# Probabilities' low halves against V's high columns only, a smaller planned cost, and 27 unread products at the end

## Chip, cores and metric

The kernel runs on one core of one Trainium2 chip. The metric is device time in microseconds, the median of several runs. Lower is better.

## The reference

Two layers, 256 positions, width 1024, one sequence. Each layer is, in short:

```python
h = rms_norm(x, gain)
proj = h @ w_in                       # 1024 -> 9808 columns, all branches at once
# qa ka va ga | qb kb vb gb | qc kc vc gc | indexer | forget logit | merge logits
oa = moba_attention(rope(qa), rope(ka), va) * silu(ga)     # 8 heads of 64
ob = dsa_attention(rope(qb), rope(kb), vb, indexer) * silu(gb)
oc = forgetting_attention(qc, kc, vc, log_f) * silu(gc)
y = stack([oa, ob, oc]) @ w_branch    # three matrices 512 -> 1024
merged = sum(sigmoid(merge_logit) * y)
x = x + merged @ w_out
```

At the end stands one more rms_norm. At 256 positions the MoBA branch is plain causal attention; the DSA branch keeps 64 keys per query; the forgetting branch adds a bias to the logits. In all three, one head computes softmax(scores) @ V with V of 64 columns.

## The kernel before

**Precision by halves.** TensorE works on fp32r operands. Every float32 operand is split into a high half (an fp32r copy, made on ACT) and a low half (the difference, made on DVE), and a product A x B is made as high x high + low x high + high x low. For V both halves lie side by side: `v[:, t, hd]` has 128 columns for head hd and key tile t, the first 64 the high half, the last 64 the low half. The transposed probabilities of a head lie in `ph` (high) and `pl` (low), 384 columns each: columns 0 to 255 are key tile 0 against all 256 queries, columns 256 to 383 key tile 1 against the last 128 queries (the rest is masked by causality).

**The attention of a pair of heads** (class Pair, function attend): scores (L566 to L568), bias, exponential and normalisation (L629 to L644), transposes of the probabilities (L656), their split (L659, L661), and then the products with V in `av` (L671 to L674). For each of the two heads, four products add into one 128 x 256 region `ov` of a PSUM bank: rows 0 to 63 collect what meets V's high columns, rows 64 to 127 what meets V's low columns. In the kernel before, the fourth product (low probabilities, key tile 0) takes all 128 columns of V, the third (low probabilities, key tile 1) only the first 64. Function gated then adds the upper and the lower 64 rows (L687 on ACT, then DVE) and multiplies by the gate. There are 3 mixers x 4 pairs x 2 layers = 24 such pairs, 48 heads.

**Projections.** Most of TensorE's work is in mm_ops (L403): weights come by DMA into three raw buffers, are split into wh (ACT, L358) and wl (DVE, L362), and are multiplied with hTh and hTl, the two halves of the transposed, normalised input. Key tiles of a pair's k are written in block form as bd (L704 on ACT, L705 on DVE).

**The order.** Nothing runs in program order. Every piece of work is an operation with an engine, a cost in ns, tokens that it reads and writes, and a key (a due number). A planner (Plan.run) simulates the engines: it takes the engine with the earliest possible start, and there the operation with the smallest key, advances that engine by the operation's cost, and emits the instruction. So the costs written into the kernel decide the order of instructions on each engine and in SP's queue of loads, not what they take on the chip. All groups of mm_ops write one token, k_main, and so keep their order among themselves; attention pieces, norms and transposes go between them as keys and planned times have it. The planned cost of `av` is 820 ns.

**The end.** The output projection w_out closes a layer. In the last layer its last part is cut in two halves of 256 columns; after each follow the residual on DVE (L1032), sum of squares, the final norm (L526 to L551) and the output's DMA. When the output has landed, SP and POOL collect all engines in a closing barrier (L1063).

Of the kernel before, what the change touches and what calls it, by code (L numbers as in the profile page):

```python
# [29 lines left out]
C_ID, C_UT, C_MASK, C_ROPE, C_END = 0, 128, 256, 640, 1664  # L30
# [11 lines left out]
MARGIN = 200.0  # L42
# [191 lines left out]
def hybrid_trunk(ctx, tc, x, norm_gain, w_in, forget_bias, w_branch, w_out, final_gain, consts, out):  # L234
    nc = tc.nc
    PE, ACT, DVE, POOL = nc.tensor, nc.scalar, nc.vector, nc.gpsimd
# [13 lines left out]
    def T(b):  # L250
        return b.slot[1]


    def pe(fn, cost, reads, writes, key, name="", margin=0.0, touch=()):
        o = plan.op([("PE", cost, fn)], reads, writes, key, 0.0, name, touch)
        o.margin = margin
        return o

    def act(fn, n, ps, reads, writes, key, name="", extra=0.0, touch=()):
        return plan.op([("ACT", t_act(n, ps) + extra, fn)], reads, writes, key, 0.0, name, touch)  # L260
# [22 lines left out]
    hTh = pool.tile([128, KC, S], F32R, name="hTh")  # L283
    hTl = pool.tile([128, KC, S], F32R, name="hTl")
# [5 lines left out]
    cst = pool.tile([128, C_END], F32, name="cst")  # L290
    ident = cst[:, C_ID:C_ID + 128]
# [17 lines left out]
    k_id, k_rope, k_gT, k_bdz, k_cst, k_fb, k_wf, k_widx, k_lf, k_cs, k_main = (Tok() for _ in range(11))  # L309
# [103 lines left out]
    hT_all = [[t for tl in k_hT[p] for t in tl] for p in range(2)]  # L413
# [158 lines left out]
    class Pair:  # L572
# [46 lines left out]
        def attend(self, key):  # L619
            bs = [self.bias(h, key) for h in range(2)]  # L620
            s0, s1 = scores(self.q, self.k, self.kt, key)
            es, ke = [], []
            for h in range(2):
                b, bt, bb = bs[h]
                e, st = Buf("e"), Buf("st")
                kt = [Tok(), Tok()]
                parts = ((0, 0, 128, s0), (1, 128, 256, s1))
                for t, a, n, s in parts:
                    dve(lambda t=t, a=a, n=n, s=s, e=e, st=st, b=b, h=h: DVE.tensor_tensor_reduce(  # L629
                        T(e)[:, a:a + n], T(s)[:, h * n:(h + 1) * n], b()[:, a:a + n], 1.0, 3e38, ALU.add, ALU.min,  # L630
                        T(st)[:, t:t + 1]), n, [s, bt[t]], [kt[t]], key, "max", touch=[e, st] + bb)
                for t, a, n, s in parts:
                    act(lambda t=t, a=a, n=n, e=e, st=st: ACT.activation(  # L633
                        T(e)[:, a:a + n], T(e)[:, a:a + n], AF.Exp, bias=T(st)[:, t:t + 1], scale=-1.0,
                        accum_out=T(st)[:, 2 + t:3 + t]), n, False, [], [kt[t]], key, "exp", 185.0, touch=[e, st])
                for t, a, n, s in parts:
                    dve(lambda t=t, st=st: DVE.reciprocal(T(st)[:, 4 + t:5 + t], T(st)[:, 2 + t:3 + t]), 1, [], [kt[t]],
                        key, "recip", 75.0, touch=[st])

                    def on_act(t=t, a=a, n=n, e=e, st=st):  # L640
                        ACT.activation(T(e)[:, a:a + n], T(e)[:, a:a + n], AF.Copy, scale=T(st)[:, 4 + t:5 + t])

                    def on_dve(t=t, a=a, n=n, e=e, st=st):
                        DVE.tensor_scalar(T(e)[:, a:a + n], T(e)[:, a:a + n], T(st)[:, 4 + t:5 + t], None, op0=ALU.mult)  # L644
                    plan.op([("DVE", 129.0 + 0.52 * n, on_dve), ("ACT", t_act(n, False) + 93.0, on_act)], [], [kt[t]],
                            key, 0.0, "normalise", touch=[e, st]).port = True
                es.append(e)
                ke.append(kt)
            ph, pl = Buf("pth"), Buf("ptl")
            kp = [[Tok(), Tok()] for _ in range(2)]  # L650
            for h in range(2):
                ps = Buf("t")

                def tr(h=h, ps=ps):
                    for i in range(3):
                        PE.transpose(T(ps)[:, i * 128:(i + 1) * 128], T(es[h])[:, i * 128:(i + 1) * 128], ident)  # L656
                pe(tr, 330.0, ke[h] + [k_id], [ps], key, "pT", MARGIN, touch=[es[h]])
                src = lambda ps=ps: T(ps)[:, :384]
                act(lambda h=h, src=src: ACT.activation(T(ph)[:, h], src(), AF.Copy), 384, True, [ps],  # L659
                    [kp[h][0]], key, "pT", touch=[ph])  # L660
                dve(lambda h=h, src=src: DVE.tensor_tensor(T(pl)[:, h], src(), T(ph)[:, h].bitcast(F32), op=ALU.subtract),  # L661
                    384, [ps, kp[h][0]], [kp[h][1]], key, "pT", touch=[ph, pl])
            o = Buf("o")
            v = V[self.vi]

            def av():
                for h in range(2):
                    hd = 2 * self.p + h
                    ov = T(o)[:, h * S:(h + 1) * S]
                    a, b = slice(0, 256), slice(256, 384)  # L670
                    PE.matmul(ov, v[:, 0, hd], T(ph)[:, h, a], start=True, stop=False)  # L671
                    PE.matmul(ov[:, 128:], v[:, 1, hd], T(ph)[:, h, b], start=False, stop=False)
                    PE.matmul(ov[:64, 128:], v[:, 1, hd, :64], T(pl)[:, h, b], start=False, stop=False)
                    PE.matmul(ov, v[:, 0, hd], T(pl)[:, h, a], start=False, stop=True)  # L674
            kv = [t for p in k_V[self.vi] for t in p]
            pe(av, 820.0, kv + [ph, pl] + [t for h in kp for t in h], [o], key, "av", MARGIN)
            self.o, self.o_key = o, key
            if hasattr(self, "g"):
                self.gated()
# [312 lines left out]
    for l in range(L):  # L992
        gates = {}
        if l == 0:
            first_v()
        else:
            v_units(l, "a", 0)
        u, ps = unit_b("kwf", lambda k: win_k(l, k), 80)
        kb, ktoks = ev_kwf(l, ps, u)
        wf_cols(l, u + 1)  # L1000

        def index_unit(p):
            u, ps = unit_b(f"qi{p}", lambda k: win_b(l, COL["qi"] + (p // 2) * 256, p % 2, k))
            index_scores(p, ps, kb, ktoks, u)
            if p == 3:
                select(u + 3, 2.0)
        first = [lambda p=p: index_unit(p) for p in range(4)] + mixer(l, "a", 0, 0)
        for f in between(first, m_of(l, 0, gates, range(8)) + m_of(l, 2, gates, range(NC1))):
            f()
        v_units(l, "c", 1)  # L1010
        for f in between(mixer(l, "c", 1, 1), alternate(y_of(l, 0, 0, 0, gates, range(8)), m_of(l, 2, gates, range(NC1, 8)))):
            f()
        v_units(l, "b", 0)
        for f in between(mixer(l, "b", 0, 0), alternate(y_of(l, 2, 1, 1, gates, range(8)), m_of(l, 1, gates, range(NB1)))):
            f()
        for f in m_of(l, 1, gates, range(NB1, 8)) + y_of(l, 1, 0, 2, gates, range(8)):
            f()
        last = l + 1 == L
        if last:
            dma(lambda: nc.sync.dma_start(acc.rearrange("p k c -> p (k c)")[:, :D],  # L1020
                                          final_gain.rearrange("(o d) -> o d", o=1).to_broadcast([128, D])),
                512 * D, [], [k_fg] + k_acc, units[0], "final gain")
        for hh in range(2):
            gets = [lambda k, i=i: rows_a("O", w_out, l, hh * 512, i, k) for i in range(4)]
            for t in range(2):
                ra = [lambda k, p=p: [k_mg[k][p]] for p in range(2)]
                cols = [(0, 256), (256, 256)] if last and hh + t == 2 else [(0, 512)]
                for i, (c, n) in enumerate(cols):
                    u, ps = unit_a(f"o{hh}{t}", gets, t, mA[0], mA[1], ra, c, n)
                    c += hh * 512  # L1030
                    o = xs[t][:, c:c + n]
                    dve(lambda o=o, ps=ps, n=n: DVE.tensor_tensor(o, o, T(ps)[:, :n], op=ALU.add), n, [ps], [k_x[t][hh]],  # L1032
                        u - 4, "res")
                    if last:
                        final_part(t, c, n, hh + i, u - 4, i == 1)
                if last and hh == 1:
                    final_norm(t, orr[t], u - 4, 1 + len(cols))
                elif hh == 1:
                    norm_to_hT(l + 1, t, u - 2)
    PLAN_T.append(plan)  # L1040
    PLAN_T[0] = plan.run({"PE": 0.0, "ACT": 0.0, "DVE": 0.0})

# [24 lines left out]
```

## Time and profile before

| | |
|---|---|
| runs | 639.62, 639.74, 640.1 us (median 639.74) |
| profiled execution, span from first to last instruction | 639.9 us |
| granted TensorE clock, mean | 0.996 |
| TensorE products (PE) / weight loads (PEld) busy | 624.9 / 595.6 us |
| DVE / ACT / POOL busy | 546.7 / 396.3 / 89.8 us |
| DMA | 105.56 MB, 165 GB/s on average |

The profiled execution's own time is known as its span alone; the three runs lie on both sides of it. Products on TensorE are pipelined, so their recorded lengths overlap: a busy share near 100% says that TensorE was never long without a product, not how fast products follow each other. What one product costs is the distance to the start of the next one.

### The profile page before, as it was taken

Reading aid. Unit: us, or ns where it says so; the run is one execution under the profiler, and the core shown is the slowest. Engines: PE = TensorE matmul, PEld = TensorE weight load, DVE = VectorE, ACT = ScalarE, POOL = GpSimd, SP = SyncE. Lnnn points to the kernel's source line nnn. Section 1 sums busy time; section 2 is a strip of 40 time slices with the busy share of each in tenths; the row PEclk is TensorE's granted clock in tenths of the full one; section 3 lists DMA queues with packets and bytes.
Section 4 is the critical chain, followed back from the end, with each engine's and each line's share of the span. In section 5 each row is a group of like instructions: output and inputs, shape, how many; then the busy total and the mean of one; then the engine's idle time right before and its main releaser. Section 6 shows DMA issues by size and latency. Waiting matters only on the chain.

```text
span 639.9 us, 12574 instructions
## 1 busy us (share of the span) xinstructions
PE 624.9 (98%) x4836; PEld 595.6 (93%) x4836; DVE 546.7 (85%) x1331; ACT 396.3 (62%) x802; POOL 89.8 (14%) x96
## 2 busy tenths in 40 slices
PE   7999989999999999999999999999999999999996
PEld 6899989999998999999889999998999889999985
DVE  7799999885969989998588999989587898999873
ACT  5675475765755658485386555767457564858641
POOL 1242131100000221200004403020000003221000
PEclk9999999999999999999999999999999999999999
DMA  8745628455382552656445634565635354552711
GB/s 292 241 142 186 198 71 291 133 165 165 104 276 84 165 173 93 198 163 233 153 134 194 198 105 160 162 201 164 205 125 198 102 171 158 165 165 99 264 34 67
DMA packets 93853, 105.56 MB, mean 165 GB/s; under 512 B 4320, under 2 KB 82400, under 8 KB 93792
## 3 DMA queue, kind: packets, MB, share of 16 engines
q1 hardware_dynamic: 93504, 104.36, 49.8%
q8 instruction: 38, 0.62, 0.4%
q10 hardware_dynamic: 288, 0.39, 0.2%
q14 instruction: 23, 0.19, 0.1%
HBM read 103.69 MB, written 1.05 MB: 164 GB/s over the span
## 4 chain that ended last, share of the span: by engine, by line
PE 82%; DVE 12%; issue 2%; ACT 2%; DMA 1%; SPq 0%; POOL 0%; POOLq 0%; DVEq 0%; ACTq 0%
PE proj L403 70%; DVE wl L362 4%; PE t L656 2%; PE proj L947 2%; PE s L566 1%; PE s L568 1%; DVE isc L801 1%; PE s L567 1%; DVE e L629 1%; PE o L674 1%; DMA x<-in_x_dram 1%; DVE t L800 1%; ACT wh L358 1%; PE o L671 1%; DVE isc L780 1%
## 5 line engine op out<-in xcount | busy, mean ns | idle before, releaser
L358 ACT ACTIVATE wh<-raw 128x1024 fp32r<-128x1024 f32 (+1 forms) x190 | 199.0, 1054 | 133.7 <-PE proj L403 107.6
L362 DVE TENSOR_TENSOR wl<-raw,wh 128x1024 fp32r<-128x1024 f32 (+1 forms) x190 | 238.4, 1264 | 39.3 <-ACT wh L358 38.3
L403 PE MATMUL proj<-hTh,wh 128*128 128x256 f32 (+1 forms) x1040 | 252.4, 278 | 1.1 <-DVE bd1l L705 0.6
L403 PE MATMUL proj<-hTl,wh 128*128 128x256 f32 (+1 forms) x1040 | 251.6, 277 | 0.0
L403 PEld LDWEIGHTS proj<-hTh,wh 128*128 128x128 f32 (+1 forms) x1040 | 194.6, 187 | 2.1 <-DVE bd1l L705 0.8
L403 PEld LDWEIGHTS proj<-hTl,wh 128*128 128x128 f32 (+1 forms) x1040 | 194.6, 187 | 0.6
L403 PE MATMUL proj<-hTh,wl 128*128 128x256 f32 (+1 forms) x1040 | 163.4, 279 | 0.0
L403 PEld LDWEIGHTS proj<-hTh,wl 128*128 128x128 f32 (+1 forms) x1040 | 139.8, 188 | 1.3
L449 POOL TENSOR_TENSOR rsh<-rsh,cst 128x256 f32<-128x256 f32 (+1 forms) x42 | 37.1, 884 | 406.4 <-DVE rsh L448 406.4
L633 ACT ACTIVATE e<-e,st 128x128 f32<-128x128 f32 x96 | 42.7, 446 | 20.0 <-DVE st L629 19.9
L451 POOL TENSOR_TENSOR rr<-rr,rsh 128x256 f32<-128x256 f32 (+1 forms) x42 | 47.5, 1131 | 15.7 <-DVE rr L450 12.9
L403 PE MATMUL proj<-wh,v 128*128 128x512 f32 (+1 forms) x144 | 35.5, 368 | 0.0
L403 PE MATMUL proj<-wh,hTh 128*128 128x512 f32 x80 | 32.7, 409 | 1.2 <-DVE bd0l L705 0.6
L403 PE MATMUL proj<-og0h,wh 128*128 128x256 f32 x128 | 32.4, 277 | 0.0
L403 PE MATMUL proj<-og0l,wh 128*128 128x256 f32 x128 | 32.3, 277 | 0.0
L403 PE MATMUL proj<-wh,hTl 128*128 128x512 f32 x80 | 31.5, 394 | 0.0
L403 PEld LDWEIGHTS proj<-wh,v 128*128 128x128 f32 x144 | 25.2, 188 | 4.7
L659 ACT ACTIVATE pth<-t 128x384 fp32r<-128x384 f32 x48 | 22.1, 484 | 8.2 <-PE t L656 8.1
L661 DVE TENSOR_TENSOR ptl<-t,pth 128x384 fp32r<-128x384 f32 x48 | 25.6, 551 | 1.5 <-ACT pth L659 1.3
L403 PE MATMUL proj<-og0h,wl 128*128 128x256 f32 x128 | 25.0, 277 | 0.0
L403 PE MATMUL proj<-wl,hTh 128*128 128x512 f32 x80 | 24.9, 392 | 0.0
L403 PEld LDWEIGHTS proj<-og0h,wh 128*128 128x128 f32 x128 | 24.1, 188 | 0.4 <-DVE mth L848 0.2
(190 smaller groups left out, 1010.7 us busy)
## 6 DMA issues: line engine op xcount, KB each, us to landing
raw<-in_w_in_dram SPq DMA_DIRECT2D x74, 1024.0 KB, 5.0
raw<-in_w_branch_dram SPq DMA_DIRECT2D x24, 512.0 KB, 3.4
raw<-in_w_out_dram SPq DMA_DIRECT2D x8, 1024.0 KB, 6.2
raw<-in_w_in_dram SPq DMA_DIRECT2D x3, 512.0 KB, 7.9
x<-in_x_dram SPq DMA_DIRECT2D x4, 256.0 KB, 5.0
raw<-in_w_in_dram SPq DMA_DIRECT2D x2, 320.0 KB, 7.0
out_dram<-tmp SPq DMA_DIRECT2D x2, 320.0 KB, 2.4
raw<-in_w_in_dram SPq DMA_DIRECT2D x2, 256.0 KB, 3.7
```

Of the source, the lines that this page charges most:

```text
L358: ACT.activation(p[0].v, sel(c.v), AF.Copy)
L362: DVE.tensor_tensor(p[1].v, sel(c.v), p[0].v.bitcast(F32), op=ALU.subtract)
L403: PE.matmul(o(), a(), b(), start=first and i == 0, stop=last and i == n - 1)
L449: gps(lambda: POOL.tensor_tensor(T(sh)[:np_], T(sh)[:np_], s[:np_], op=ALU.mult), S, [k_rope], [sh], key, "rope")
L451: gps(lambda: POOL.tensor_tensor(T(r)[:np_], T(r)[:np_], T(sh)[:np_], op=ALU.add), S, [sh], [r], key, "rope")
L566: PE.matmul(o, qh[:, sl], kh[:, :, :n], start=True, stop=False)
L567: PE.matmul(o, ql[:, sl], kh[:, :, :n], start=False, stop=False)
L633: act(lambda t=t, a=a, n=n, e=e, st=st: ACT.activation(T(e)[:, a:a + n], T(e)[:, a:a + n], AF.Exp, bias=T(st)[:, t:t + 1], scale=-1.0, acc ...
L656: PE.transpose(T(ps)[:, i * 128:(i + 1) * 128], T(es[h])[:, i * 128:(i + 1) * 128], ident)
L659: act(lambda h=h, src=src: ACT.activation(T(ph)[:, h], src(), AF.Copy), 384, True, [ps], [kp[h][0]], key, "pT", touch=[ph])
L661: dve(lambda h=h, src=src: DVE.tensor_tensor(T(pl)[:, h], src(), T(ph)[:, h].bitcast(F32), op=ALU.subtract), 384, [ps, kp[h][0]], [kp[h][1 ...
L947: PE.matmul(T(ps[t]), h(2 * i + x, t), v3(w)[:, x], start=left[t][0] == 23, stop=left[t][0] == 0)
```

## The change

Three edits.

1. In `av` the fourth product (low probabilities, key tile 0) meets only the first 64 columns of V, its high half, and so writes only rows 0 to 63 of `ov`. The third product did so already. The contribution low x low, which rows 64 to 127 got from key tile 0, is no longer made. As rows 64 to 127 now end with the second product, the stop flag stands there as well, and all four products carry skip_group_check. Number and moving width of the products stay: 256, 128, 128 and 256 columns.
2. The planned cost of `av` goes from 820 to 700 ns.
3. A new function `pace` adds one operation for TensorE behind the last group of mm_ops (it reads k_main, and its key of one million is larger than any other). It makes 27 products into three PSUM buffers (tags s, s, t) that nobody reads: five with 32 weight columns and 512 moving columns, five with 32 and 256, five with 128 and 512, six with 128 and 256, two in plain float32 (the identity against 512 columns of the constants), and four of 64 rows, in turn the lower and the upper half of the partitions, with 128 and 256. Its planned cost is 6000 ns.

```diff
-                    PE.matmul(ov, v[:, 0, hd], T(ph)[:, h, a], start=True, stop=False)
-                    PE.matmul(ov[:, 128:], v[:, 1, hd], T(ph)[:, h, b], start=False, stop=False)
-                    PE.matmul(ov[:64, 128:], v[:, 1, hd, :64], T(pl)[:, h, b], start=False, stop=False)
-                    PE.matmul(ov, v[:, 0, hd], T(pl)[:, h, a], start=False, stop=True)
+                    PE.matmul(ov, v[:, 0, hd], T(ph)[:, h, a], start=True, stop=False, skip_group_check=True)
+                    PE.matmul(ov[:, 128:], v[:, 1, hd], T(ph)[:, h, b], start=False, stop=True, skip_group_check=True)
+                    PE.matmul(ov[:64, 128:], v[:, 1, hd, :64], T(pl)[:, h, b], start=False, stop=False, skip_group_check=True)
+                    PE.matmul(ov[:64], v[:, 0, hd, :64], T(pl)[:, h, a], start=False, stop=True, skip_group_check=True)
             kv = [t for p in k_V[self.vi] for t in p]
-            pe(av, 820.0, kv + [ph, pl] + [t for h in kp for t in h], [o], key, "av", MARGIN)
+            pe(av, 700.0, kv + [ph, pl] + [t for h in kp for t in h], [o], key, "av", MARGIN)
...
+    def pace():
+
+        b = [Buf(t) for t in "sst"]
+        mv = lambda n, k=0: hTl.rearrange("p k c -> p (k c)")[:, k * 256:k * 256 + n]
+
+        def emit():
+            b0, b1, b2 = (T(x) for x in b)
+            for i in range(5):
+                PE.matmul(b0[:32], hTh[:, i, :32], mv(512, i), start=True, stop=True)
+            for i in range(5):
+                PE.matmul(b0[:32, :256], hTh[:, i, :32], mv(256, i), start=True, stop=True)
+            for i in range(5):
+                PE.matmul(b1, hTh[:, i + 2, :128], mv(512, i), start=True, stop=True)
+            for i in range(6):
+                PE.matmul(b0[:, :256], hTh[:, i, :128], mv(256, i), start=True, stop=True)
+            for i in range(2):
+                PE.matmul(b2, ident, cst[:, C_ROPE:C_ROPE + 512], start=True, stop=True)
+            for i in range(4):
+                r = slice(64 * (i % 2), 64 * (i % 2) + 64)
+                PE.matmul((b0, b1)[i % 2][:, :256], hTh[r, i, :128], mv(256, i)[r], start=True, stop=True)
+        pe(emit, 6000.0, [k_main] + hT_all[0] + hT_all[1] + [k_id, k_rope], b, 10 ** 6, "pace")
+    pace()
```

## Prediction

> **What bounds the kernel now.** I read the page's busy times and slices first, then what TensorE waited for, then the stages.
>
> ```profile
> span 639.9 us, 12574 instructions
> ...
> PE 624.9 (98%) x4836; PEld 595.6 (93%) x4836; DVE 546.7 (85%) x1331; ACT 396.3 (62%) x802; POOL 89.8 (14%) x96
> ...
> PE 82%; DVE 12%; issue 2%; ACT 2%; DMA 1%; SPq 0%; POOL 0%; POOLq 0%; DVEq 0%; ACTq 0%
> ```
> ```profile
> PE s L568 <- DVE bd1l L705: 1.6, 1, 1.6
> PE proj L403 <- DVE bd0l L705: 1.2, 2, 0.6
> ...
> PE proj L403 <- DVE bd2l L705: 0.6, 1, 0.6
> PE proj L403 <- DVE bd1l L705: 0.6, 1, 0.6
> PE t L656 <- ACT e L641: 0.4, 2, 0.3
> ```
> ```profile
> 50.00:92.00 42.00, 39.92 (x335) 38.74 (x334) 41.51 (x127) 23.61 (x46) 11.89 (x12) 1.00 0.48 154
> 92.00:160.00 68.00, 67.93 (x540) 65.17 (x539) 55.25 (x115) 43.71 (x90) 3.89 (x4) 1.00 0.55 179
> ...
> 560.00:594.00 34.00, 34.00 (x297) 33.68 (x295) 32.75 (x81) 23.41 (x53) 5.70 (x6) 1.00 0.42 138
> ```
>
> The first fence is the page: TensorE is busy in 98% of the span and carries 82% of the chain that ended last. The second lists who waited for whom (total us, times, longest): TensorE's waits in the steady part come to a few microseconds, and the four on DVE's bd writes are 0.6 us each. The third gives stages: window and its length, then busy time of PE, PEld, DVE, ACT and POOL, granted clock, DMA share and GB/s. From 92 us on TensorE is filled and its clock is 1.00, so a nanosecond less of its work shortens the run unless another engine is equally full. DVE nearly is in places: 32.75 of 34 us from 560 on. From 50 to 92 us DVE is the bound (41.51 of 42 us).
>
> **The change, part 1: 64 instead of 128 weight columns in the fourth product.** One attention pair (function av) makes four products for each of two heads, at L671 to L674. These are their records over the whole run (minimum/median/maximum ns), and one pair in order of time (start us, length us):
>
> ```profile
> L671 PE MATMUL o<-pth,v x48: 276/279/363, 91.8 to 593.7; 128*128 128x256 f32 x48
> L673 PEld LDWEIGHTS o<-ptl,v x48: 133/134/136, 91.9 to 593.9; 128*64 128x64 f32 x48
> L674 PEld LDWEIGHTS o<-ptl,v x48: 187/188/188, 92.0 to 593.9; 128*128 128x128 f32 x48
> L674 PE MATMUL o<-ptl,v x48: 330/332/336, 92.0 to 594.0; 128*128 128x256 f32 x48
> ```
> ```profile
> 91.78 0.28 PE L671 MATMUL o<-pth,v 128*128 128x256 f32 x1
> 91.89 0.22 PE L672 MATMUL o<-pth,v 128*128 128x128 f32 x1
> 91.95 0.22 PE L673 MATMUL o<-ptl,v 128*64 128x128 f32 x1
> 92.01 0.33 PE L674 MATMUL o<-ptl,v 128*128 128x256 f32 x1
> 92.18 0.28 PE L671 MATMUL o<-pth,v 128*128 128x256 f32 x1
> ...
> 92.59 0.28 PE L403 MATMUL proj<-hTh,wh 128*128 128x256 f32 x1
> ```
>
> Lengths overlap, so the cost is the distance between starts. A product over 256 columns costs 0.11 us (91.78 to 91.89), one over 128 columns 0.06 (91.89 to 91.95 to 92.01). L674 has 256 columns as well, but costs 0.17 us (92.01 to 92.18). Its record says the same: 332 ns against 279 for the equally wide L671. The 53 ns stand in all 48 records (330 to 336). A pair as a whole takes 92.59 - 91.78 = 0.81 us.
>
> Why L674 stalls: its weights are 128 columns wide, and what runs while they load is L673, which gives only 0.06 us of cover. How long a load of 128 columns holds the port shows where almost nothing is multiplied:
>
> ```profile
> 38.93 0.31 PEld L754 LDWEIGHTS t<-fz,cst 128*128 128x128 f32 x2
> 39.15 0.30 PEld L755 LDWEIGHTS t<-fz,cst 128*128 128x128 f32 x2
> ```
>
> These serve products of 8 columns and still come two in 0.22 us (38.93 to 39.15), 0.11 each. So 0.11 against a cover of 0.06 leaves 0.05 us open: the stall of L674. A load of 64 columns is recorded 54 ns shorter (134 against 188), and behind L672, as short as L673, it fits without a stall (L673 starts 0.06 after L672). With 64 columns L674 should start 0.06 after L673, cost 0.11, and the next head's 128-column load has a 256-column product as cover, as every L403 product has. Saving: 48 x 0.054 us = 2.6 us. Its lower end is nothing (the second rival below); above, it cannot exceed the 48 x 0.06 = 2.9 us by which L674 lies over L671.
>
> One share is lost. The chain of waits still runs on DVE and ACT when the first pair is made at 91.78 us, and comes over to TensorE only behind this piece (start us, length us):
>
> ```profile
> 96.53 0.40 ACT e L641
> ```
>
> TensorE waits there for ACT's e (one of the two L656 waits above, 0.3 us at most), and that wait eats the first pair's 0.11 us. I count 2.5 us.
>
> The new start and stop flags add no instruction and cost nothing.
>
> **Part 2: the planner is told 700 instead of 820 ns for a pair.** The kernel orders every engine's instructions by simulated due times, so all later decisions can move, the weight loads in SP's queue too, though no DMA is added. Both figures are true ones: 0.81 us measured before, and 0.81 - 0.11 = 0.70 after. So the plan fits the chip as well as it did, and I take zero for the reordering. Its ends: the main products follow each other in a fixed order by one token, so only the attention pieces and the ACT and DVE work shift. At best the four 0.6 us waits close (-2.4 us); at worst each of the six mixers gets one more such wait (+3.6 us).
>
> **Part 3: 27 products behind the last projection (pace).** Nothing reads them and nothing is queued behind them on TensorE except the closing barrier. They read banks s, s, t and tiles whose last users are long done, so I count their waits at nothing. What matters is whether they outlast the tail on the other engines.
>
> ```profile
> 624.62 0.62 PE L403 MATMUL proj<-wl,v 128*128 128x512 f32 x2
> ...
> 626.01 0.62 PE L403 MATMUL proj<-wl,v 128*128 128x512 f32 x2
> ...
> 632.82 0.64 PE L403 MATMUL proj<-wh,v 128*128 128x256 f32 x4
> 633.29 0.40 PE L403 MATMUL proj<-wl,v 128*128 128x256 f32 x2
> ```
> ```profile
> 199.88 0.66 PE t L656 x6
> ```
> ```profile
> L862 PE MATMUL t<-ones x28: 275/421/581, 1.1 to 6.7; 128*128 128x128 f32 x28
> ```
> ```profile
> L1063 PEldq DRAIN  x2: 13/1163/2313, 631.4 to 639.5; - x2
> L1063 POOLq EVENT_SEMAPHORE  x4: 17/17/17, 639.2 to 639.8; - x4
> ```
>
> Six products of 512 columns take 1.39 us (624.62 to 626.01), 0.232 each; four of 256 take 0.47 (632.82 to 633.29), 0.118 each. A float32 pass over 128 columns costs 0.11 (six L656 in 0.66), so 0.44 over 512; a plain float32 product leaves two records (28 at L862 for WARM = 14 calls), so 0.88. Pace holds ten of 512 columns (2.32), eleven of 256 (1.30), two float32 of 512 (1.76) and four of 256 on half the rows (0.47): 5.85 us. It starts behind the last projection product (the second of the row at 633.29, so 633.41 + 0.12 = 633.53), issues its last at about 639.3, and has its result at 639.54, since a 256-column product's record ends 0.16 after its slot (0.28 against 0.12). Before, TensorE's drain was over at 631.4 + 2.31 = 633.7, and the closing barrier began to collect the engines at 639.2, once the output had landed. So 5.5 us of pace are free, covered by the final norm and the output DMA. Pace overruns the cover by 639.54 - 639.2 = 0.34, plus some hundredths for its drain: I take +0.4 us.
>
> Bounds: nothing, if the float32 products go at the 512-column price of 0.232; and about +2.0 if they go at the L862 price (28 records from 1.1 to 6.7 us, 0.21 apart, so 0.42 for a call over 128 columns and 1.7 over 512: 1.6 more for the two). The L656 row is nearest, because it stands among projections, as pace stands behind them.
>
> The Trainium skill, TensorE: Matmul & The Clock Gate, Part 3, holds that products on different row groups run side by side; the last four of pace alternate between rows 0 to 63 and 64 to 127. By that rule two of the four slots vanish (2 x 0.118), and pace overruns by 0.2 instead of 0.4. No row here has two half-height products in turn, so I keep the rows' price.
>
> **The sum.** -2.5 (part 1) + 0 (part 2) + 0.4 (part 3) = -2.1 us. The profiled execution's span is 639.9 us, 0.2 above the median of 639.74 and inside the runs' 639.62 to 640.1; taken off the median this gives 637.6 us, 0.33% faster. About 0.2% (1.3 us) is what a measurement of this kernel tells from no change.
>
> **The rivals.**
>
> 1. *DVE takes back part of the gain.* Where DVE has 32.75 of 34 us, a shorter TensorE stretch leaves it less slack, and new waits on its bd, e and pt writes appear. For it: that row. Against it: even there 1.2 us are left, and a pair gives only 0.11. If half of 2.5 us is lost: 638.9 us, within 0.2%. Chance 0.15.
>
> 2. *The stall is not the load's width but the return from 64 to 128 columns.* Then it moves from L674 to whatever follows it, and only pace is left: 639.74 + 0.4 = 640.1. For it: L674 is just the product where the width returns. Against it: entering the narrow product at L673 costs nothing extra, and 0.05 us is what the 0.11 load spacing predicts. The Trainium skill, TensorEngine Tiling (Array Packing), Key Properties, says that a change of the tiling mode drains the engine. By that rule each head has two changes before and two after, and the gain would be nil; the entry into L673 does not show such a drain. Chance 0.10.
>
> 3. *Slower: the new order costs a wait in each mixer.* Planned times move by 0.12 us a pair, a wl split slips ahead of a bd write on DVE, and the scores or the next projection wait for it. One 0.6 us wait in each of six mixers is 3.6 us: 637.6 + 3.6 = 641.2. It decides from about 3.4 us on; two waits like the 1.6 us at L568, one per layer, give 640.8 and are not enough. For it: such waits are there already, and the two layers repeat each other, so one bad decision counts twice. Chance 0.13.
>
> 4. *Faster than forecast: the new order closes the four 0.6 us waits.* 637.6 - 2.4 = 635.2. Chance 0.12.
>
> **How the numbers follow.** The forecast keeps 0.50, with its own range from 636.6 (pace hidden, some waits shorter) to 638.6 (float32 at half as much again as the L656 price). Rivals 1 and 2 end within 0.2%, as does a little of the forecast's upper edge and rival 3's lower part; rival 4 and most of the forecast are faster, with the better part of rival 1. Faster 0.63, same 0.25, slower 0.12. The range 635.4 to 640.4 reaches over rivals 1 and 2, most of 4 and the bounds of pace, and leaves rival 3 out.
>
> **What would show it.** Part 1: L674's record falls from 332 to about 278 ns, its load from 188 to 134, and from L671's first start to the product after the pair are 0.70 us; if rival 2 holds, the next product's record carries the 53 ns. Part 2: the list of TensorE's waits keeps four bd waits of about 0.6 us. Part 3: TensorE is busy to the end, the drain ends last of all engines, and from the last projection product to the end of the span are 6.9 instead of 6.5 us. The forecast is wrong if the waits on DVE grow by over 1 us, or if pace runs over 6.5 us.

## The result, and the profile after

The changed kernel takes 635.87 us (635.52 to 637.72, five runs) against 639.74 us (638.82 to 640.35); the ratio is 0.9942, 95% interval 0.9921 to 0.9963. Measured a second time it gave 636.3 against 639.93 us, ratio 0.9944 (0.9928 to 0.9959). So it is 3.6 to 3.9 us faster. The forecast was 637.6: the direction was right, and the time is inside the stated range, but below the forecast's own range of 636.6 to 638.6.

In some executions the granted clock falls to half for 3.4 us from 12.4 to 13.2 us on, which makes them 1.5 to 2 us longer; both profiled executions are of this kind, so their start is left out of the comparison. A run's time is 1.8 us over its span (637.51 against 635.7 for the profiled one).

The page of the changed kernel:

```profile
span 635.7 us, 12647 instructions
...
PE 626.8 (99%) x4865; PEld 595.1 (94%) x4865; DVE 545.0 (86%) x1327; ACT 396.0 (62%) x802; POOL 93.0 (15%) x100
...
PE 85%; DVE 11%; ACT 1%; issue 1%; DMA 1%; POOL 0%; SPq 0%; DVEq 0%
```

TensorE stays the bound. Busy time rises although the kernel is shorter, because the 27 products at the end are counted. Whom TensorE waited for (total us, times, longest):

```profile
PE s L568 <- DVE bd1l L705: 1.6, 1, 1.6
...
PE proj L403 <- DVE bd0l L705: 1.2, 2, 0.6
...
PE proj L403 <- DVE bd2l L705: 0.6, 1, 0.6
PE proj L403 <- DVE bd1l L705: 0.6, 1, 0.6
PE t L656 <- ACT e L641: 0.5, 2, 0.4
```

Behind the start the list is that of before to 0.1 us: the four bd waits of 0.6 us are there, none is added. The fourth product over the whole run (minimum/median/maximum ns), and one pair in order of time (start us, length us):

```profile
L674 PEld LDWEIGHTS o<-ptl,v x48: 134/135/139, 90.9 to 591.5; 128*64 128x64 f32 x48
L674 PE MATMUL o<-ptl,v x48: 279/281/282, 91.0 to 591.5; 128*64 128x256 f32 x48
```
```profile
176.60 0.28 PE L671 MATMUL o<-pth,v 128*128 128x256 f32 x1
...
177.13 0.22 PE L673 MATMUL o<-ptl,v 128*64 128x128 f32 x1
177.19 0.28 PE L674 MATMUL o<-ptl,v 128*64 128x256 f32 x1
177.31 0.28 PE L403 MATMUL proj<-hTh,wh 128*128 128x256 f32 x1
177.43 0.28 PE L403 MATMUL proj<-hTl,wh 128*128 128x256 f32 x1
```

L674's record fell from 332 to 281 ns and its distance to the next product from 0.17 to 0.12 us; the pair takes 0.71 us instead of 0.81. The width returns to 128 columns at 177.31 and nothing stalls there.

Where the 53 ns were lost shows in the loads alone, in the trace of before:

```profile
178.61 0.19 PEld L674 LDWEIGHTS o<-ptl,v 128*128 128x128 f32 x1
178.72 0.19 PEld L671 LDWEIGHTS o<-pth,v 128*128 128x128 f32 x1
```

Where nothing stalls, a load in these pairs starts 2 to 4 ns behind the start of the product ahead of it. Here the next load waits until 178.72, 0.05 us behind the start of L674 at 178.67, because the load of L674 came only 0.11 us before.

The end, from the chain that ended last, and the closing barrier (L1085 here):

```profile
629.10 1.16 PE s L1048 x5
630.26 0.58 PE s L1050 x5
630.85 1.16 PE s L1052 x5
632.00 0.71 PE s L1054 x6
632.72 1.72 PE t L1056 x4
634.44 0.43 PE s L1059 x4
```
```profile
L1085 SPq EVENT_SEMAPHORE  x7: 17/28/420, 632.0 to 635.6; - x7
L1085 POOLq EVENT_SEMAPHORE  x4: 17/17/17, 635.0 to 635.6; - x4
```

Now the chain ends on TensorE. SP's longest wait in the barrier is 0.42 us (it was 28 ns at most in the trace of before), and that is the overrun of the unread products. From the last projection product to the end of the span are 6.88 instead of 6.50 us.

What none of the forecast's steps contains shows in the projection products behind a pair. One piece of the chain of before, and the same 96 products after:

```profile
179.41 11.15 PE proj L403 x96
```
```profile
177.47 10.91 PE proj L403 x96
```

The same work, 0.24 us shorter. Product by product, 256-column projection products start either 113 to 114 ns or 117 to 119 ns apart, in long stretches of one or the other, with hardly anything between. The changed kernel has more of the short distance. The table counts the long ones (116 to 130 ns) from 20 us on, among some 3640 distances up to 130 ns between neighbouring L403 products, worked out from their starts in one trace of each kernel. "Behind a pair" are those from a pair to the next work of another kind or the next pause; the last column adds up what all distances have over 113 ns:

| kernel | fourth product's columns | long behind a pair | long elsewhere | excess, us |
|---|---|---|---|---|
| before | 128 | 491 of 1494 | 774 of 2144 | 7.0 |
| e1, end products alone | 128 | 581 of 1495 | 805 of 2144 | 7.6 |
| e10, ahead of its series | 128 | 722 of 1495 | 766 of 2144 | 8.2 |
| e3, cost alone | 128 | 576 of 1330 | 859 of 2306 | 7.7 |
| e5, first head narrow | 64 and 128 | 502 of 1326 | 941 of 2308 | 7.8 |
| e6, second head narrow | 128 and 64 | 572 of 1329 | 722 of 2308 | 7.2 |
| e7, third product twice | 128 | 764 of 1506 | 753 of 2134 | 8.2 |
| e9, other order | 128 | 603 of 1481 | 687 of 2144 | 7.2 |
| changed kernel, twice | 64 | 87 and 85 of 1330 | 875 and 869 of 2306 | 5.6, 5.6 |
| e4, change without end products | 64 | 85 of 1330 | 894 of 2306 | 5.7 |
| e2, columns alone | 64 | 62 of 1302 | 707 of 2330 | 4.8 |
| e8, 96 columns | 96 | 95 of 1305 | 772 of 2330 | 5.2 |
| e11, columns and filled start | 64 | 58 of 1338 | 660 of 2298 | 4.7 |

No kernel with a full 128-column fourth product in either head is below 7.0, none without one above 5.7. The difference lies behind the pairs: there 33 to 51% of the distances are long in the first eight kernels and 4 to 7% in the others, while elsewhere the shares are alike (31 to 41% and 29 to 39%).

This accounts for the time. From the first pair's first product to the last projection product the three traces with the attention and the order of before (before, e1, and e10 ahead of its series) take 541.63, 542.11 and 542.66 us, those of the changed kernel (twice) and of e4 538.09, 537.95 and 538.07: 4.1 us less in the mean. The pairs themselves are 2.5 us of it, the rest is in the projection products. With the 0.4 us at the end this makes -3.7, against the -3.9 and -3.6 measured. The experiments below belong to these rows.

### The profile page after: what moved, and what is told of

The parts are those of the page before. It is cut to its first block, busy times and chain, and to the rows that moved or that the text cites. A ratio compares the mean times of both kernels' runs of the same rounds, so it can differ in the third digit from the quotient of the medians.

```text
span 635.7 us, 12647 instructions
## 1 busy us (share of the span) xinstructions
PE 626.8 (99%) x4865; PEld 595.1 (94%) x4865; DVE 545.0 (86%) x1327; ACT 396.0 (62%) x802; POOL 93.0 (15%) x100
## 4 chain that ended last, share of the span: by engine, by line
PE 85%; DVE 11%; ACT 1%; issue 1%; DMA 1%; POOL 0%; SPq 0%; DVEq 0%
PE proj L403 72%; DVE wl L362 4%; PE t L656 3%; PE proj L947 2%; PE s L566 1%; PE s L568 1%; PE s L567 1%; DVE isc L801 1%; DVE t L800 1%; DVE e L629 1%; PE o L674 1%; PE o L671 1%; ACT wh L358 1%; DVE isc L780 1%; PE t L611 1%
## 5 line engine op out<-in xcount | busy, mean ns | idle before, releaser
L403 PE MATMUL proj<-hTh,wh 128*128 128x256 f32 (+1 forms) x1040 | 252.5, 278 | 1.1 <-DVE bd1l L705 0.6
L403 PE MATMUL proj<-hTl,wh 128*128 128x256 f32 (+1 forms) x1040 | 251.2, 277 | 0.0
L403 PEld LDWEIGHTS proj<-hTh,wh 128*128 128x128 f32 (+1 forms) x1040 | 194.5, 187 | 2.4 <-DVE bd1l L705 0.8
L403 PEld LDWEIGHTS proj<-hTl,wh 128*128 128x128 f32 (+1 forms) x1040 | 194.6, 187 | 0.7
L403 PE MATMUL proj<-hTh,wl 128*128 128x256 f32 (+1 forms) x1040 | 162.7, 279 | 0.0
L403 PEld LDWEIGHTS proj<-hTh,wl 128*128 128x128 f32 (+1 forms) x1040 | 139.4, 187 | 1.3
L451 POOL TENSOR_TENSOR rr<-rr,rsh 128x256 f32<-128x256 f32 (+1 forms) x42 | 45.9, 1092 | 15.7 <-DVE rr L450 12.9
L403 PE MATMUL proj<-wh,v 128*128 128x512 f32 (+1 forms) x144 | 35.6, 368 | 0.0
L403 PE MATMUL proj<-wh,hTh 128*128 128x512 f32 x80 | 32.7, 409 | 1.2 <-DVE bd2l L705 0.6
L403 PE MATMUL proj<-og0h,wh 128*128 128x256 f32 x128 | 32.2, 276 | 0.0
L403 PE MATMUL proj<-og0l,wh 128*128 128x256 f32 x128 | 32.2, 276 | 0.0
L403 PE MATMUL proj<-wh,hTl 128*128 128x512 f32 x80 | 31.5, 394 | 0.0
L403 PEld LDWEIGHTS proj<-wh,v 128*128 128x128 f32 x144 | 25.2, 188 | 4.7
L403 PE MATMUL proj<-og0h,wl 128*128 128x256 f32 x128 | 24.9, 276 | 0.0
L403 PE MATMUL proj<-wl,hTh 128*128 128x512 f32 x80 | 24.9, 392 | 0.0
L403 PEld LDWEIGHTS proj<-og0h,wh 128*128 128x128 f32 x128 | 24.0, 188 | 0.2
```

Source lines behind the costliest of these rows:

```text
L403: PE.matmul(o(), a(), b(), start=first and i == 0, stop=last and i == n - 1)
L451: gps(lambda: POOL.tensor_tensor(T(r)[:np_], T(r)[:np_], T(sh)[:np_], op=ALU.add), S, [sh], [r], key, "rope")
```

## The experiments

**e1 to e4: each part of the change by itself.** They ran on one chip against the same 23 runs of before (640.1 us median).

e1, the kernel before plus the end:

```diff
...
+    pace()
```

> The kernel before plus the 27 unread products alone. The forecast's term: +0.4 us (640.1 against 639.7), with SP waiting about 0.4 us for TensorE in the closing barrier, since the order of everything else is untouched. Rival, that the products cost nothing because the output DMA hides them: 639.7 and no such wait. A third theory, that a busy end of one execution changes the granted clock at the start of the next, would show as a time below 639 us and as another record of the clock in the first 20 us.

Measured: 639.98 us, ratio 1.0003 (0.999 to 1.0017), so +0.2 us with an interval from -0.6 to +1.1. The time cannot tell 0.4 from 0; the trace can:

```profile
L1085 SPq EVENT_SEMAPHORE  x7: 17/28/417, 636.7 to 640.3; - x7
```

The barrier waits 0.417 us for TensorE, as forecast. The theory of another clock at the next start falls: the median is not below 639, and the half clock stands in this kernel's trace as well.

e2, the narrow fourth product alone (the flags of the other three are those of the change):

```diff
-                    PE.matmul(ov, v[:, 0, hd], T(pl)[:, h, a], start=False, stop=True)
+                    PE.matmul(ov[:64], v[:, 0, hd, :64], T(pl)[:, h, a], start=False, stop=True, skip_group_check=True)
```

> The fourth product with 64 weight columns (so low probabilities no longer meet V's low columns in key tile 0) and the flags alone; planned cost stays 820, no products at the end. All orders are those of before. If the whole steady gain is the uncovered weight load: 48 x 0.053 = 2.5 us, 637.2. If the planned cost carries a part of it (about 1 us of the traces' difference), the same 637.2 here, but the full change without the end products then lies about 1 us lower. If the stall only moves to another product: 639.7.

Measured: 635.9 us, ratio 0.9933 (0.9919 to 0.9947), that is -4.3 us (-5.2 to -3.4). With the order unchanged on every engine, this one edit gives the whole gain, and more than the 2.5 us of its own stall.

e3, the cost alone:

```diff
-            pe(av, 820.0, kv + [ph, pl] + [t for h in kp for t in h], [o], key, "av", MARGIN)
+            pe(av, 700.0, kv + [ph, pl] + [t for h in kp for t in h], [o], key, "av", MARGIN)
```

> Planned cost 700 instead of 820 alone, with the wide fourth product and nothing at the end; the plan is then 0.11 us too short for each of 24 pairs. Forecast's term: 0, so 639.7. Theory that the new order is worth about 1 us in the stretch from 92 to 628 us: 638.7, with fewer or shorter waits there than before. Theory that a plan which promises too much costs: above 640.

Measured: 639.85 us, ratio 1.0002 (0.999 to 1.0013). The order on TensorE, DVE, ACT and POOL changes in many places and is worth nothing that the times show (-0.6 to +0.8 us): the forecast's zero holds.

e4, the change without the end products:

> The change without the 27 unread products (low probabilities of key tile 0 still leave V's low columns out). Forecast's sum without +0.4: 637.2; if the order is worth another 1 us: 636.2. It should lie 0.4 us below the changed kernel. If the end products were what made several executions of the changed kernel 1.7 us shorter at the start, this kernel has none of those short ones and lies near 637.2 or above.

Measured: 636.0 us, ratio 0.9937 (0.9922 to 0.9952). It cannot be told from e2, so the order brings nothing on top; nor from the changed kernel, against which 0.4 us was expected. Short executions occur here too (down to 634.98), so the end products do not make them.

**e5 and e6: one head of two.** The surplus of e2 over its stalls was 1.8 us. The fourth product was narrowed in one head only (the flags as in the change):

```diff
+                    n = 64 if h == 0 else 128      # e6: h == 1
+                    PE.matmul(ov[:n], v[:, 0, hd, :n], T(pl)[:, h, a], start=False, stop=True, skip_group_check=True)
```

> Only the first head of each pair gets the fourth product with 64 weight columns (there the low probabilities of key tile 0 leave V's low columns out); the second head keeps 128. Planned cost 820, no end products, order as before. Theory A: the gain has two parts, 53 ns at each of 48 wide products (2.5 us), and about 2 us more because the projection products that follow a pair whose last product stalled run at 117 to 119 ns instead of 113 to 114. Then this half removes 24 x 53 ns = 1.3 us and leaves the after-effect: 638.8, and the products behind a pair stay about 2 ns slower on average. Theory B, both heads count alike: half of 4.2, 638.0. Theory C, only the stalls count and the rest was spread between runs: 638.8 with products behind a pair as in any other kernel.

> Only the second head of each pair gets 64 weight columns in its fourth product (low probabilities of key tile 0 leave V's low columns out there). Theory A: 1.3 us from the stalls and the whole after-effect of 2 us, since the pair's last product no longer stalls: 636.9, and the products behind a pair average about 113.6 ns. Theory B: 638.0. Theory C: 638.8.

Measured, against 640.7 us: 639.18, ratio 0.9978 (0.9966 to 0.9991), and 639.0, ratio 0.9978 (0.9968 to 0.9988), both -1.4 us. Half the stalls (1.3 us) are gained in each, and nothing else: two halves make 2.8, not 4.3. The intervals alone would not tell these apart; the table does, with 38 and 43% of the distances behind a pair still long. So theory C describes each half, theory A fails in e6 (it gave the whole after-effect to the pair's last product), and theory B, equal shares of the whole, fails in both. The faster projection products appear only when no head has a full-width fourth product.

**e7: a second product as cover.**

```diff
                     PE.matmul(ov[:64, 128:], v[:, 1, hd, :64], T(pl)[:, h, b], start=False, stop=False)
+                    PE.matmul(ov[:64, 128:], v[:, 1, hd, :64], T(pl)[:, h, b], start=False, stop=False)
```

> The kernel before with the third product made twice (so key tile 1's low probabilities count twice), which puts a second short product as cover ahead of the wide fourth load. The load of 0.11 us then has 0.12 us of cover; the extra product costs about 0.058, the stall of 0.053 goes. If an uncovered load is what stalls and what slows the products behind (theory A): +0.2 - 2.0 = about 638.3, the fourth product's record near 280 ns and the products behind at about 113.6 ns. If the stall comes from the return from 64 to 128 columns: the record stays at 332 ns and the time rises by 48 x 0.058 = 2.8 us to 642.9. If the products behind are slow because short products come in a row: stall gone, slow products as before or more, 640.3 or above.

Measured: 642.32 us, ratio 1.0034 (1.0021 to 1.0047), +2.2 us by the ratio and 1.6 by the medians. The copy (L674 here) and the wide product (L675) over the run:

```profile
L674 PE MATMUL o<-ptl,v x48: 222/223/224, 89.4 to 595.1; 128*64 128x128 f32 x48
L675 PE MATMUL o<-ptl,v x48: 329/332/334, 89.5 to 595.2; 128*128 128x256 f32 x48
```

The stall stays at 332 ns; theory A's 638.3 is missed, and the run looks like the second rival of the prediction. But it could also be that a load starts only when the product just ahead has begun, so that two short products cover no more than one. The loads of one pair have it so:

```profile
177.60 0.13 PEld L674 LDWEIGHTS o<-ptl,v 128*64 128x64 f32 x1
177.65 0.19 PEld L675 LDWEIGHTS o<-ptl,v 128*128 128x128 f32 x1
177.76 0.19 PEld L403 LDWEIGHTS proj<-hTh,wh 128*128 128x128 f32 x1
```

The wide load starts at 177.65 together with the copy, not earlier, and again the next load comes 0.11 us behind it. e8 and e9 put the two readings to the test.

**e8: 96 columns** (the flags as in the change).

```diff
+                    PE.matmul(ov[:96], v[:, 0, hd, :96], T(pl)[:, h, a], start=False, stop=True, skip_group_check=True)
```

> The fourth product with 96 weight columns (low probabilities of key tile 0 meet half of V's low columns). A load of 96 columns should take 0.08 us against 0.058 of cover: 0.022 to 0.027 us of stall left at each of 48, the record near 305 ns, 1.3 to 1.5 us gained from stalls. If any uncovered load slows what follows: 638.3 to 638.8 and the products behind a pair as before; if the after-effect shrinks with the stall: 637.5.

```profile
L674 PE MATMUL o<-ptl,v x48: 303/306/312, 89.5 to 589.3; 128*96 128x256 f32 x48
```

The record is 306 ns: half the stall for half the surplus width, as 0.027 us per 32 columns of load predicts. From this load's start to that of the next are 82 ns in the median, against 108 with 128 columns. The cost belongs to the load's width. The time is 636.04 us, ratio 0.9935 (0.9922 to 0.9948), -4.2 us, below all three expectations: half of the stalls remains, yet the products behind run as fast as with 64 columns (95 of 1305 long). The trace accounts for 3.0 of the 4.2 us: from the first pair to the last projection product it takes 539.10 us, against 542.13 in the mean of the three above.

**e9: two exposed loads per head.**

```diff
                     PE.matmul(ov, v[:, 0, hd], T(ph)[:, h, a], start=True, stop=False)
-                    PE.matmul(ov[:, 128:], v[:, 1, hd], T(ph)[:, h, b], start=False, stop=False)
+                    PE.matmul(ov, v[:, 0, hd], T(pl)[:, h, a], start=False, stop=False)
                     PE.matmul(ov[:64, 128:], v[:, 1, hd, :64], T(pl)[:, h, b], start=False, stop=False)
-                    PE.matmul(ov, v[:, 0, hd], T(pl)[:, h, a], start=False, stop=True)
+                    PE.matmul(ov[:, 128:], v[:, 1, hd], T(ph)[:, h, b], start=False, stop=True)
```

> The kernel before with the same four products of each head in another order: first product, then the wide fourth, then the third (64 weight columns), then the second (128 weight columns, 128 moving), so that two loads of 128 columns per head come behind a product of 0.058 us: the second product's, and the one of the product that follows the head. If what counts is the load against the one product ahead of it: two stalls of 0.053 us per head instead of one, +2.5 us, the second product's record near 275 instead of 221 ns and the fourth's at 279. If what counts is the return from 64 to 128 weight columns: one such return per head as before, time unchanged, and only the second product's record grows.

The first, the wide fourth (L672 here) and the second product (L674 here):

```profile
L671 PE MATMUL o<-pth,v x48: 276/331/365, 89.6 to 593.8; 128*128 128x256 f32 x48
L672 PE MATMUL o<-ptl,v x48: 276/279/283, 89.7 to 594.0; 128*128 128x256 f32 x48
L674 PE MATMUL o<-pth,v x48: 272/273/278, 89.9 to 594.2; 128*128 128x128 f32 x48
```

The stalls sit where the load theory puts them: the wide product behind a 256-column one has none (279 ns); the second product, of 128 columns behind 0.06 us, has 52 ns (273 against 221 before); and so has the product that follows a head (331 for the second head's first one), where no width changes at all. So the rival of the width's return falls, and with it the drain as an explanation of this stall. The time, however, is 639.87 us, ratio 1.0004 (0.9993 to 1.0015), not +2.5. The profiled execution was the longest of its twelve (641.62), and from the first pair to the last projection product it takes 543.74 us, against 541.63 to 542.66 with the order of before: there the added stalls are paid, at least in part. Why the median of twelve does not show them is not settled.

**e10: the disputed distances by themselves.** Eight unread series at the end of the kernel before, when nothing else works.

> The kernel before with eight unread series at the end, about 9 us each, where no other engine and no DMA works: 16 products of 128 x 256, two heads' worth of attention products, and 48 products of 128 x 256 to be read for their distance; the fourth product has 128/128, 64/64, 96/96, 128/64, 64/128 columns in the two heads, and the first three again. If a wide fourth product by itself slows what follows: the 48 products take 48 x 0.118 = 5.65 us behind 128/128, 128/64 and 64/128, and 48 x 0.1135 = 5.45 behind 64/64 and 96/96. If the slow distance needs the traffic of the other engines, all eight take the same. The stalls themselves (0.17, 0.144 and 0.118 us for the fourth product) should stand here as in the kernel.

The 48 products (L1055) and the second head's fourth (L1053), behind 128/128, 64/64 and 96/96 columns:

```profile
634.82 0.33 PE L1053 MATMUL s<-hTl,hTh 128*128 128x256 f32 x1
634.98 5.92 PE L1055 MATMUL t<-hTl,hTh 128*128 128x256 f32 x48
...
643.26 0.28 PE L1053 MATMUL s<-hTl,hTh 128*64 128x256 f32 x1
643.38 5.92 PE L1055 MATMUL t<-hTl,hTh 128*128 128x256 f32 x48
...
651.68 0.30 PE L1053 MATMUL s<-hTl,hTh 128*96 128x256 f32 x1
651.82 5.92 PE L1055 MATMUL t<-hTl,hTh 128*128 128x256 f32 x48
```

The fourth products stall as in the kernel (0.33, 0.28, 0.30 us). The products behind take the same 5.92 us in all series, about 0.120 us each: nearly all at the long distance (373 of 376 at 116 ns or more). So the series do not reproduce the two distances, and say neither that a stall causes the long one nor that it doesn't. They differ from the kernel in two things at once, the operands (here the weights are slices of hTh) and the absence of other engines' work.

**e11: a version that goes further.** e2, and eight unread products in the wait for the second weight chunk:

```diff
+                            if i == 0 and t == 0 and h is hA[1] and j == (1,):
+                                for _ in range(8):
+                                    PE.matmul(fill[:, :128], ones, ones, start=True, stop=True)
```

> The narrow fourth product alone (planned cost 820, nothing at the end; low probabilities of key tile 0 leave V's low columns out) and eight unread float32 products of 128 columns in the wait for the second weight chunk at 9 us, where TensorE stands still for 2 us and the granted clock falls to half for 3.4 us in some executions. If the wait is set by the loads alone and the clock falls for the idle time: no execution with the half clock at 12 to 16 us, the median 0.5 to 1 us below the narrow product alone (about 635.2), and less spread. If the clock falls for another reason: as the narrow product alone, 635.9.

The start without (e2) and with the filling (L952):

```profile
8.79 0.63 PE L947 MATMUL proj<-wh,hTl 128*128 128x512 f32 x2
11.07 0.70 PE L947 MATMUL proj<-wh,hTh 128*128 128x512 f32 x2 [1.65 <-DVE wh L937]
```
```profile
9.01 0.63 PE L949 MATMUL proj<-wh,hTl 128*128 128x512 f32 x2
9.48 1.95 PE L952 MATMUL proj<-ones 128*128 128x128 f32 x16
11.27 0.71 PE L949 MATMUL proj<-wh,hTh 128*128 128x512 f32 x2
```

Measured: 635.2 us (634.69 to 635.46), ratio 0.9922 (0.9909 to 0.9936); none of its five runs is 1 us above another. It has the lowest median here, 1.1 us below the changed kernel on the same chip (636.3), which the intervals do not quite separate. The spread fits the theory that idle time makes the clock fall; with five runs this is not shown, and the two traces cannot decide, since neither has the half clock near 13 us.

e12 is the changed kernel again.

> The changed kernel once more, on the same chip as the three above and with the same runs of the kernel before. Forecast's -2.1 us would be 638; the narrow product alone gave -4.2 on its chip, and the end products add 0.4 in the trace: -3.8, so a ratio of 0.994.

Measured: 636.3 us, ratio 0.9944 (0.9928 to 0.9959), as given above.

## Why the prediction was right in direction and short in size

- **Part 1, the stall of the fourth product (-2.5 us): right, but not the whole of the term.** Distances from L674 to the next product fell from 170.3 to 118.6 ns on average, 48 x 51.7 = 2.5 us; whether the one pair that was counted as lost is lost is below what these runs resolve. The cause, a 128-column load behind one 0.06 us product, is borne out by the loads' starts, e8 and e9. The term that was mis-sized is the same edit's total: alone it gives -4.3 us (-5.2 to -3.4, e2). The working took the products behind a pair as unchanged, though the trace of before holds two distances for them; of those behind a pair 33 to 48% were long with the kernel before's attention and order and 6 to 7% are in the changed kernel. That is the missing part: in the traces 4.1 us instead of 2.5. Why a full-width load left uncovered keeps the following products at 118 ns stays open: e5 and e6 show that one such load per pair is enough, e9 that it need not be the fourth product's, e8 that a load with half the stall is not enough.
- **Part 2, the new order (0): right.** e3 measures 1.0002, and the four bd waits stay as they were, so rivals 3 and 4 did not come about.
- **Part 3, the end products (+0.4): right in the trace** (0.42 us of waiting in the barrier), too small for the times. From the first start to the last result the 27 products take 5.93 us, 0.08 less than forecast. The float32 products take 1.72 us (1.76 forecast). The four half-height products start in pairs, as the Trainium skill, TensorE: Matmul & The Clock Gate, Part 3, has it, and the trace agrees: at distances of 3 to 4 ns within a pair. But the second pair starts 0.22 us behind the first, not 0.12, and ahead of the first TensorE stands for 0.09 us, so that of the 0.24 us which that rule promised 0.03 are left.
- **Rival 1 (DVE takes gain back)** did not occur: its waits are unchanged. **Rival 2 (return of the width)** is refuted by e8 and e9. The drain that the Trainium skill, TensorEngine Tiling (Array Packing), Key Properties, states for a change of tiling mode is not seen between 64 and 128 weight columns, if that is such a change: the way in costs 0.06 us a product, the way back 0.12, both without a stall when the load is covered.
- **The profiled execution against the median.** The prediction set its span beside the times of the runs. A run's time is 1.8 us over its span, so the profiled one (639.9 + 1.8 = 641.7) was longer than all of them. The sum was taken off the median, so this moved nothing.
- **The range.** That it holds the time is in part luck: its lower end was drawn for rival 4, the closing of the four 0.6 us waits, and those waits stand as before. The time came near rival 4's 635.2 by another way.

## What to carry to other kernels

Read TensorE's cost from start to start, and compare each weight load with the one product directly ahead of it: here a load of 128 columns keeps the next load waiting for about 0.11 us, so behind a product of 128 moving columns half of that was lost; narrowing the load (e2) or putting a wider product ahead (e9) removed it, while a second short product (e7) did not. When a chain of thousands of equal products makes the time, look at the spread of their distances, not at one of them: here 4 ns each, in stretches, were worth more than half as much as a stall that could be pointed at. A planner's cost that moves hundreds of instructions can be worth nothing where the same engine stays full (e3).

## What was not expected of the hardware

Equal 256-column products have two steady distances, 113 to 114 and 117 to 120 ns, at a granted clock of 1.00; behind a pair a full-width load left uncovered makes the long one frequent, and what sets it is not settled here. A pause of TensorE of 1.6 us near 9 us precedes a half clock of 3.4 us in some executions of the changed kernel and not in others, worth 1.5 to 2 us.
